# A fixed order for the first two SSD chunks, and other staging buffers for late weights, in a hybrid SSD and attention block

## The chip, the cores and the metric

The kernel runs on one NeuronCore of one Trainium2 chip. The metric is device time in microseconds of one launch, the median of several. The core has five instruction streams that run side by side: TensorE (PE in the profile, its weight loads PEld), VectorE (DVE), ScalarE (ACT), GpSimd (POOL) and SyncE (SP), which issues most DMAs. Each engine takes its instructions strictly in the order in which they stand in its queue, and waits on semaphores for the others.

## The reference

One encoder layer over a sequence of 1024 rows of width 1024, batch 1, all float32. The input is normalised and modulated (scale and shift from a conditioning vector), then one projection feeds two mixers of width 512 each: a Mamba-2 SSD group and a chunked attention group. Their outputs are concatenated, go through W_out, are gated and added; a feed-forward block with a depthwise convolution follows, then a last norm. The change is in the SSD mixer and in what surrounds it:

```python
xbc = jax.nn.silu(causal_dwconv(xbc, conv_w) + conv_b)      # x (512), B (256), C (256)
dt = jax.nn.softplus(dt_raw + dt_bias);  A = -jnp.exp(a_log)
y = ssd_scan(xs * dt[..., None], dt * A, bm, cm)            # decay masks exp(segment sums), states
y = y + d_skip[:, None] * xs
y = y.reshape(b, s, SSD_WIDTH) * jax.nn.silu(z)
y_ssd = rmsnorm(y, norm_w)
x = x + g_m * (jnp.concatenate([y_ssd, y_att], axis=-1) @ w_out)
```

## The kernel before

Float32 products run as three fp32r matmuls of a high and a low part (mm3); the function split makes the two parts of a tile, the high one on ScalarE and the low one on VectorE. After attention come the convolutions of x, B and C (tiles xst, bt, ct), then z's projection in two passes of 260 columns (ch 1, then ch 0), eight row tiles of 128 each, then the SSD in eight chunks of 128 rows.

**z.** wz_weights(ch) loads a pass's weights in four pieces into the two halves of raws (raw_tile hands them out in turn) and splits each into wzh and wzl, of which there are four buffers, so a pass's pieces are replaced as the pass before ends. z_mm makes a row tile (24 matmuls), z_evac writes zs. Between the tiles of the second pass stand, in an order written by hand, the preparation of the decays (dt_prep: sm_p, sm_e, sm_t, dt, adh and adl; dt_sums: running sums on TensorE, tile tp), the masks of chunks 0 and 1, and the splits of W_out's eight slots (wout_split, tiles hH and hL), staged in wos and raws.

**SSD.** For a chunk, pre_x scales x (xdt, xdd), pre_rm makes the decay mask's operands (tile rm, two buffers, "mask buffers"), pre_sg sums them on TensorE (sg), pre_cb makes C times B and B's transpose (xps to cb), and pre_m takes the exponential of sg on ScalarE and multiplies by cb on VectorE (tile th). ssd_y then makes y: on TensorE ydp (from th and xdt), yop (from the state) and stp (the next state), on VectorE the sum of ydp and GpSimd's yy, the products with the decays and with zs; ScalarE squares it, GpSimd makes the root, ScalarE scales y, and ssd_turn transposes it back into xs, which is half of W_out's input. wout_half(n) multiplies one half of a row tile by W_out (tile wops; n even is attention's half, from ya, n odd the SSD's, from xs), after wout_rhs has split that half into yhl. In chunk c the half c fills TensorE's time while the masks of chunk c+1 are made.

**What sets the order.** TensorE's order from z's second pass to the last chunk is that of the code. On VectorE and ScalarE a scheduler in the compiler sets the order, by its own estimate of the times; only where V.on and A.on are set does every instruction come after the one before it in the code. Before the change that part ends inside chunk 0: the two engines' instructions after ssd_y(0) are the scheduler's. GpSimd and SP are always the scheduler's.

```python
y = ssd_y(c, *pre)
V.on = A.on = False
if turn:
    ssd_turn(*turn)
```

Of the kernel before, what the change touches and what calls it, by code (L numbers as in the profile page):

```python
# [10 lines left out]
F32 = mybir.dt.float32  # L11
F32R = mybir.dt.float32r
# [4 lines left out]
P = 128  # L17
# [47 lines left out]
def tile_block(ctx: ExitStack, tc: tile.TileContext, x, crep, pk, w_ada, w_first, w_ft, w_z,  # L65
# [14 lines left out]
    def split(hi, lo, src, ehi, elo, scale=None):  # L80
        if scale is not None:
            A.activation(hi, src, AF.Copy, scale=scale)
            V.scalar_tensor_tensor(lo, src, scale, f32(hi), op0=ALU.mult, op1=ALU.subtract)
            return
        i = A.activation(hi, src, AF.Copy) if ehi is A else ehi.tensor_copy(hi, src)  # L85
        return i, elo.tensor_tensor(lo, src, f32(hi), ALU.subtract)  # L86
# [19 lines left out]
    def stat(n=1):  # L106
        if stc[0] + n > 64:
            stc[0] = 0
        a = st1[:, stc[0]:stc[0] + n]
        stc[0] += n  # L110
        return a

    def rstd(ms, eps=EPS):
        n = ms.shape[-1]
        r = stat(n)
        G.tensor_scalar(ms, ms, eps, None, op0=ALU.add)
        G.tensor_tensor(r, ms, mhalf[:, 0:n], ALU.pow)
        return r
# [8 lines left out]
    def raw_tile(n=1024):  # L127
        rawc[0] += 1
        return raws[:, rawc[0] % 2, 0:n]
# [499 lines left out]
    def wz_weights(ch):  # L629
        ws = []  # L630
        for a in range(4):
            th_ = wzp.tile([P, 2, 288], F32R, tag="wzh", bufs=WZB, name="wzh")[:, :, 0:260]
            tl_ = wzp.tile([P, 2, 288], F32R, tag="wzl", bufs=WZB, name="wzl")[:, :, 0:260]
            t = raw_tile(520)
            nc.sync.dma_start(t, w_z[ch, :, a * 520:(a + 1) * 520])
            split(th_, tl_, t.rearrange("p (a b) -> p a b", a=2), A, V, scale=0.5)
            ws.append((th_, tl_))
        return ws

    def z_mm(ch, st, wz):  # L640
        if st % 4 > 1:
            ps = psv.tile([P, 512], F32, tag=("acc", "pv")[st % 4 - 2], bufs=1, name="zps")[:, 0:260]
        else:
            ps = s_tile()[:, 0:260]
        for kt in range(KT):
            mm3(ps, hth[st // 4][:, st % 4, kt, :], htl[st // 4][:, st % 4, kt, :],
                wz[kt // 2][0][:, kt % 2, :],
                wz[kt // 2][1][:, kt % 2, :], kt == 0, kt == KT - 1)
        return ps
# [121 lines left out]
    def wout_get(*slots):  # L771
        for j in slots:
            wt[j] = wout_load(*WORDER[j])
# [11 lines left out]
            wout_fold(wt[j])  # L785
    wz = wz_weights(0)
    wout_get(5, 2)
    V.on = A.on = T.on = True
    V.last = A.last = T.last = None
    zp = z_mm(0, 0, wz)  # L790
# [56 lines left out]
    def sg_tile():  # L847
        return ps2a.tile([P, 512], F32, tag="seg", bufs=PB[2], name="sg")
# [4 lines left out]
    def ssd_y(c, xdt, xdd, cb, ms_):  # L853
        cs = slice(c * P, (c + 1) * P)
        prev, cur = state[c % 2], state[(c + 1) % 2]
        ydp = ssd_tile("ydp")
        for h in range(8):
            pe(T.matmul, ydp[:, h * 64:h * 64 + 64], ms_[h // 4][:, h % 4, :],
               xdt[:, h * 64:h * 64 + 64], start=True, stop=True)
        y = sp.tile([P, 512], F32, tag="yy", bufs=2, name="yy")  # L860
        G.tensor_tensor(h8(y), h8(xs[:, c, :]),
                        pkt[:, DSK:DSK + 8].unsqueeze(2).to_broadcast([P, 8, 64]), ALU.mult)
        t = sp.tile([P, 512], F32, tag="yt", bufs=2, name="yt")
        if c > 0:
            yop = ssd_tile("yop")
            for g in range(2):
                pe(T.matmul, yop[:, g * 256:g * 256 + 256], ct_[g][:, cs], prev[:, g * 256:g * 256 + 256],
                   start=True, stop=True)
        if c < NT - 1:
            stp = ssd_tile("stp")  # L870
            for g in range(2):
                pe(T.matmul, stp[:, g * 256:g * 256 + 256], cb[:, 2 + g, :],
                   xdd[:, g * 256:g * 256 + 256], start=True, stop=True)
            if c > 0:
                G.tensor_tensor(h8(cur), h8(prev), hb("cd", c), ALU.mult)
                V.tensor_tensor(cur, stp, cur, ALU.add)
            else:
                A.activation(cur, stp, AF.Copy)
        V.tensor_tensor(y, ydp, y, ALU.add)
        if c > 0:  # L880
            V.tensor_tensor(h8(t), h8(yop), hb("ea", c), ALU.mult)
            V.tensor_tensor(y, y, t, ALU.add)
        V.tensor_tensor(y, y, zs[:, c, 0:512], ALU.mult)
        ms = stat()
        A.activation(t, y, AF.Square, accum_out=ms)
        r = rstd(ms, 512.0 * EPS)
        A.activation(y, y, AF.Copy, scale=r)
        return y

    def ssd_turn(c, y):  # L890
        tps = x_tile()
# [17 lines left out]
            for j, g in enumerate(names):  # L909
                gd[g, m] = t[:, :, j, :]  # L910

    mod_scale(affn, SC_F, NFFN, 0, KT)
    mod_shift(bffn, SH_F, 0, KT)
    xr_, yq, wps, xrs = {}, {}, {}, []

    def wout_rhs(st, part):
        if st < NT:
            y = yq[st, part] = wu.tile([P, 2, 4, P], F32R, tag="wh", name="yhl")
            split(y[:, 0], y[:, 1], x1[part][:, st, :].rearrange("p (a b) -> p a b", a=4), A, V)

    def wout_half(n, ks=slice(0, 8), fill=()):
        st, part = n // 2, n % 2
# [58 lines left out]
    pre, turn = pre0, None  # L981
    T.on = False
    chain[:] = [T.last]
    for c in range(NT):
        y = ssd_y(c, *pre)
        V.on = A.on = False
        if turn:
            ssd_turn(*turn)
        turn = (c, y)
        if c < NT - 1:  # L990
            pre = ssd_pre(c + 1, x_tile, sg_tile, lambda: wout_half(c, slice(0, 3)),
                          pre1 if c == 0 else None)
            row_scale(pin[0])
            wout_half(c, slice(3, 8))
        else:
            wout_half(c)
# [565 lines left out]
```

## Time and profile before

| | us |
|---|---|
| median of three runs (1216.84 to 1219.11) | 1217.25 |
| profiled execution, its own time | 1217.67 |
| its span, first to last instruction | 1215.9 |
| z's first pass ends, second begins | 394.6 |
| z's second pass ends, chunk 0 begins | 423.7 |
| chunk 2 begins | 451.0 |

The times in the profile count from the span's start. In a timeline row stand the start, the duration, the engine, the line, the operation and its tiles, and in brackets how long the engine had been idle and what released it; L58 is the helper that holds the order written by hand, so there the tile tells the place. A row of waits reads: engine and tile, the engine and tile waited for, total time, times, longest. In a table of stretches the clock is TensorE's granted clock, 1.00 being full speed.

### The profile page before, as it was taken

The numbers are of one execution on the slowest core, as the hardware profiler recorded it, in microseconds if no ns is written. First come the engines' busy times: TensorE is split into PE (matmuls) and PEld (weight loads), VectorE is DVE, ScalarE is ACT, GpSimd is POOL, SyncE is SP. The second block draws the span as 40 slices with busy tenths as digits, with TensorE's granted clock in tenths as the row PEclk, the third lists the DMA queues.
The fourth block names the chain that finished last, engine by engine and source line by source line (L and its number), as shares of the span: only waits on it lengthen the run. The fifth ranks groups of instructions, "written<-read, shape, count | busy, mean of one in ns | idle before, by whom it ended". The sixth has DMA issues, their size and how long they took to land.

```text
span 1215.9 us, 15656 instructions
## 1 busy us (share of the span) xinstructions
PE 1162.3 (96%) x5802; PEld 976.8 (80%) x5802; DVE 942.3 (77%) x1413; ACT 594.9 (49%) x1001; POOL 195.2 (16%) x174
## 2 busy tenths in 40 slices
PE   5999999999999989999899999999999999999995
PEld 4887888778889978888688888888888888888884
DVE  7756455598697788747899988988889779766976
ACT  4637465663333657676454543444434445433443
POOL 1109373782210134200000000000000000000002
PEclk9999999999999999999999999999999999999998
DMA  9632121323554301141223223322333278733533
GB/s 355 237 94 83 36 74 39 129 81 127 174 174 157 104 18 36 61 147 53 70 80 129 96 104 130 118 81 87 105 130 112 91 265 293 261 118 125 169 117 138
DMA packets 56683, 151.91 MB, mean 125 GB/s; under 512 B 5664, under 2 KB 5792, under 8 KB 55200
## 3 DMA queue, kind: packets, MB, share of 16 engines
q1 hardware_dynamic: 49552, 126.54, 31.3%
q10 hardware_dynamic: 7056, 24.38, 5.0%
q8 instruction: 45, 0.74, 0.3%
q14 instruction: 30, 0.25, 0.1%
HBM read 117.61 MB, written 29.10 MB: 121 GB/s over the span
## 4 chain that ended last, share of the span: by engine, by line
PE 67%; DVE 7%; ACT 2%; DMA 1%; issue 1%; POOL 0%; DVEq 0%; POOLq 0%; SPq 0%; ACTq 0%
PE dn L76 6%; PE dn L77 6%; PE dn L78 6%; PE wops L702 6%; PE uY L76 5%; PE uY L78 5%; PE uY L77 5%; PE uZ L78 3%; PE uZ L77 3%; PE uZ L76 3%; PE uX L78 3%; PE uX L77 3%; PE uX L76 3%; PE s L76 2%; PE s L77 2%; PE s L78 2%
## 5 line engine op out<-in xcount | busy, mean ns | idle before, releaser
L978 POOL TENSOR_TENSOR st<-st,mhalf 128x1 f32<-128x1 f32 x16 | 12.7, 799 | 691.7 <-DVE st L977 680.3
L76 PE MATMUL dn<-w 128*128 128x512 f32 x308 | 111.9, 389 | 0.0
L77 PE MATMUL dn<-w 128*128 128x512 f32 x308 | 111.9, 389 | 0.0
L78 PE MATMUL dn<-w 128*128 128x512 f32 x308 | 103.3, 389 | 0.0
L76 PE MATMUL uY<-tH,w 128*128 128x512 f32 x256 | 99.7, 390 | 1.8 <-ACT w L58 1.8
L410 POOL TENSOR_SCALAR p<-p,st 128x640 f32<-128x640 f32 (+4 forms) x64 | 98.5, 1554 | 13.6 <-DVE st L409 10.4
L78 PE MATMUL uY<-tH,w 128*128 128x512 f32 x256 | 99.6, 389 | 0.0
L77 PE MATMUL uY<-tL,w 128*128 128x512 f32 x256 | 99.6, 389 | 0.0
L85 ACT ACTIVATE w<-ya 128x1024 fp32r<-128x1024 f32 (+1 forms) x41 | 39.1, 955 | 86.1 <-PE uY L78 80.8
L702 PE MATMUL wops<-hH,yhl 128*128 128x512 f32 x224 | 74.9, 403 | 2.6 <-ACT yhl L85 1.4
L78 PEld LDWEIGHTS dn<-w 128*128 128x128 f32 x308 | 57.8, 188 | 12.1
L76 PEld LDWEIGHTS dn<-w 128*128 128x128 f32 x308 | 57.8, 188 | 12.0
L77 PEld LDWEIGHTS dn<-w 128*128 128x128 f32 x308 | 57.8, 188 | 11.9
L85 ACT ACTIVATE pt<-tp 128x512 fp32r<-128x512 f32 (+2 forms) x72 | 36.6, 523 | 48.6 <-PE tp L436 19.7
L404 DVE CUSTOM_DVE_ANT_0 p<-s,bias 128x640 f32<-128x640 f32 (+4 forms) x64 | 40.6, 650 | 25.4 <-PE tp L439 8.5
L86 DVE TENSOR_TENSOR pt<-tp,pt 128x512 fp32r<-128x512 f32 (+2 forms) x72 | 41.9, 595 | 22.3 <-ACT pt L85 13.4
L76 PEld LDWEIGHTS uY<-tH,w 128*128 128x128 f32 x256 | 48.0, 188 | 12.1 <-ACT w L58 2.2
L77 PEld LDWEIGHTS uY<-tL,w 128*128 128x128 f32 x256 | 48.1, 188 | 10.0
L78 PEld LDWEIGHTS uY<-tH,w 128*128 128x128 f32 x256 | 48.1, 188 | 9.9
L85 ACT ACTIVATE w<-xs 128x1024 fp32r<-128x1024 f32 (+1 forms) x41 | 38.9, 952 | 32.4 <-PE uY L78 32.4
L702 PEld LDWEIGHTS wops<-hH,yhl 128*128 128x128 f32 x224 | 42.4, 191 | 11.9 <-ACT yhl L85 1.7
L76 PE MATMUL s<-hH,wh 128*128 128x512 f32 x128 | 50.6, 395 | 0.9 <-DVE ct L515 0.9
(472 smaller groups left out, 3426.8 us busy)
## 6 DMA issues: line engine op xcount, KB each, us to landing
gz<-a ACTq DMA_DIRECT2D x10, 1024.0 KB, 5.3
wos<-in_w_ada_dram SPq DMA_DIRECT2D x18, 512.0 KB, 4.1
ya<-in_w_up_dram SPq DMA_DIRECT2D x11, 768.0 KB, 4.2
xs<-in_w_up_dram SPq DMA_DIRECT2D x11, 768.0 KB, 4.4
adat<-in_w_ada_dram SPq DMA_DIRECT2D x16, 512.0 KB, 6.4
raws<-in_w_ft_dram SPq DMA_DIRECT2D x16, 512.0 KB, 3.6
qk<-in_w_ada_dram SPq DMA_DIRECT2D x14, 512.0 KB, 4.4
gy<-a ACTq DMA_DIRECT2D x10, 512.0 KB, 2.6
```

Of the source, the lines that this page charges most:

```text
L76: T.matmul(ps, lh, rh, start=start, stop=False, skip_group_check=more)
L77: T.matmul(ps, lh, rl, start=False, stop=False, skip_group_check=more)
L78: T.matmul(ps, ll, rh, start=False, stop=stop, skip_group_check=more)
L85: i = A.activation(hi, src, AF.Copy) if ehi is A else ehi.tensor_copy(hi, src)
L86: return i, elo.tensor_tensor(lo, src, f32(hi), ALU.subtract)
L404: V.tensor_tensor_reduce(out=dst, in0=src, in1=bsl, scale=-1.0, scalar=3e38, op0=ALU.add, op1=ALU.min, accum_out=nm)
L410: G.tensor_scalar(pv_, pv_, rr, None, op0=ALU.mult)
L702: i = op(*a, **k)
L978: G.tensor_tensor(r, ms, mhalf[:, 0:1], ALU.pow)
```

## The change

Four edits, all between the convolutions and chunk 2.

1. z's second pass stages its pieces 2 and 3 in the mask buffers (tag rm, name wzt) instead of the raws halves that pieces 0 and 1 use.
2. The three small operations that make affn and bffn stand earlier in the code, where the scheduler still sets the order.
3. The split of attention's first half (wout_rhs(0, 0)) joins the order written by hand, before slot 5's; slots 6 and 7 of W_out leave it there and come in chunk 0, behind parts of y.
4. Chunks 0 and 1 are written out in a fixed order for VectorE and ScalarE too. y's square and scale are separate functions, so that the exponential of the next chunk's first mask can stand ahead of the square; chunk 0 is turned inside its own chunk, its W_out half is cut at 3 and 6; in the fixed part the state's sum comes after y's.

```diff
+            if ch == 0 and a > 1:
+                t = bcp.tile([P, S], F32, tag="rm", bufs=2, name="wzt")[:, 0:520]
+            else:
+                t = raw_tile(520)
...
+    mod_scale(affn, SC_F, NFFN, 0, KT)
+    mod_shift(bffn, SH_F, 0, KT)
...
     zp = z_mm(0, 7, wz)
+    wout_rhs(0, 0)
     wout_split(5, wt[5])
     z_evac(0, 7, zp)
-    for j in (6, 7):
-        wout_split(j, wt[j])
...
+    def ssd_sq(y, t):
         ms = stat()
         A.activation(t, y, AF.Square, accum_out=ms)
-        r = rstd(ms, 512.0 * EPS)
+        return rstd(ms, 512.0 * EPS)
+
+    def ssd_scale(y, r):
         A.activation(y, y, AF.Copy, scale=r)
         return y
...
-    for c in range(NT):
-        y = ssd_y(c, *pre)
-        V.on = A.on = False
+    y, t = ssd_y(0, *pre)
+    wout_split(6, wt[6])
+    sg = pre_sg(pre1[0], sg_tile())
+    cb = pre_cb(1, x_tile())
+    wout_half(0, slice(0, 3))
+    m0 = pre_m(0, sg, cb)
+    r = ssd_sq(y, t)
+    wout_split(7, wt[7])
+    sg = pre_sg(pre1[1], sg_tile())
+    y = ssd_scale(y, r)
+    m1 = pre_m(1, sg, cb)
+    pre = *pre1["x"], cb, [m0, m1]
+    pre2 = {"x": pre_x(2), 0: pre_rm(2, 0)}
+    wout_half(0, slice(3, 6))
+    ssd_turn(0, y)
+    wout_rhs(0, 1)
+    pre2[1] = pre_rm(2, 1)
+    wout_half(0, slice(6, 8))
+    y, t = ssd_y(1, *pre)
+    sg = pre_sg(pre2[0], sg_tile())
+    cb = pre_cb(2, x_tile())
+    wout_half(1, slice(0, 3))
+    m0 = pre_m(0, sg, cb)
+    r = ssd_sq(y, t)
+    sg = pre_sg(pre2[1], sg_tile())
+    m1 = pre_m(1, sg, cb)
+    turn = 1, ssd_scale(y, r)
+    V.on = A.on = False
+    pre = *pre2["x"], cb, [m0, m1]
+    wout_half(1, slice(3, 8))
+    for c in range(2, NT):
+        y = ssd_norm(*ssd_y(c, *pre))
         if turn:
             ssd_turn(*turn)
```

ScalarE where z's first pass ends and the second begins, before (zt is z_evac's, wzh the weights, sm_e and na dt_prep's):

```order
L654 ACTIVATE zt<-zps 128x260
L82 ACTIVATE wzh<-raws 128x2x260 x2
L654 ACTIVATE zt<-zps 128x260
L82 ACTIVATE wzh<-raws 128x2x260
L58 ACTIVATE sm_e<-sm_p 128x64
L58 ACTIVATE na<-pkt 128x8
L82 ACTIVATE wzh<-raws 128x2x260
L58 ACTIVATE adh<-sm_e 128x64
```

and with the change:

```order
L657 ACTIVATE zt<-zps 128x260
L82 ACTIVATE wzh<-raws 128x2x260 x2
L82 ACTIVATE wzh<-wzt 128x2x260
L657 ACTIVATE zt<-zps 128x260
L82 ACTIVATE wzh<-wzt 128x2x260
L58 ACTIVATE sm_e<-sm_p 128x64
L58 ACTIVATE na<-pkt 128x8
L58 ACTIVATE adh<-sm_e 128x64
```

The two late pieces stand ahead of dt_prep's first exponential, and no longer on both sides of it.

VectorE from the last z tile on, before (hL slots 6 and 7 of W_out, cb and th the masks of chunk 1, yy the y of chunk 0):

```order
L58 SCALAR_TENSOR_TENSOR zs<-zt,zps 128x260
L709 TENSOR_TENSOR xdt<-xs,sm_dt 128x512
L58 SCALAR_TENSOR_TENSOR hL_86<-wos,pkt,hH_84 128x512 x2
L719 TENSOR_TENSOR rm<-tle_2879,adl 128x512
L58 SCALAR_TENSOR_TENSOR hL_86<-raws,pkt,hH_84 128x512
L740 TENSOR_TENSOR cb<-xps,tle_2879 128x512
L58 SCALAR_TENSOR_TENSOR hL_86<-raws,pkt,hH_84 128x512
L58 TENSOR_TENSOR st_72<-modc,pkt 128x8
L748 TENSOR_TENSOR th<-th,cb 128x512 x2
L58 SCALAR_TENSOR_TENSOR affn<-st_72,pkt 128x8
L58 TENSOR_TENSOR bffn<-modc,pkt 128x8
L58 TENSOR_TENSOR yy<-ydp,yy 128x512
```

and with the change:

```order
L58 SCALAR_TENSOR_TENSOR zs<-zt,zps 128x260
L58 TENSOR_TENSOR yy<-ydp,yy 128x512
L58 TENSOR_TENSOR yy<-yy,zs 128x512
L58 SCALAR_TENSOR_TENSOR hL_86<-wos,pkt,hH_84 128x512 x2
L58 TENSOR_TENSOR cb<-xps,tle_2879 128x512
L58 TENSOR_TENSOR th<-th,cb 128x512
L58 SCALAR_TENSOR_TENSOR hL_86<-raws,pkt,hH_84 128x512 x2
L58 TENSOR_TENSOR th<-th,cb 128x512
L58 TENSOR_TENSOR xdt<-xs,sm_dt 128x512
L58 TENSOR_TENSOR rm<-tle_2879,adl 128x512
L58 TENSOR_TENSOR yhl<-xs,yhl 128x512
```

y of chunk 0 comes first and slots 6 and 7 after it, between the masks; xdt and rm of chunk 2 come after the masks of chunk 1.

ScalarE in chunk 0, before (state the chunk's state, th<-sg the exponentials, yt the square and the second yy the scale of y):

```order
L58 ACTIVATE hH_84<-wos,pkt 128x512 x2
L58 ACTIVATE hH_84<-raws,pkt 128x512 x2
L58 ACTIVATE state_4137<-stp 128x512
L747 ACTIVATE th<-sg 128x512
L717 ACTIVATE rm<-tle_2879,adh 128x128 x4
L747 ACTIVATE th<-sg 128x512
L717 ACTIVATE rm<-tle_2879,adh 128x128 x4
L723 ACTIVATE rm<-tle_2879,adl 128x128 x4
L58 ACTIVATE yt,st_72<-yy 128x512
L58 ACTIVATE yy<-yy,st_72 128x512
```

and with the change:

```order
L58 ACTIVATE state_4137<-stp 128x512
L58 ACTIVATE hH_84<-wos,pkt 128x512 x2
L58 ACTIVATE th<-sg 128x512
L58 ACTIVATE yt,st_72<-yy 128x512
L58 ACTIVATE hH_84<-raws,pkt 128x512 x2
L58 ACTIVATE yy<-yy,st_72 128x512
L58 ACTIVATE th<-sg 128x512
L58 ACTIVATE rm<-tle_2879,adh 128x128 x4
L58 ACTIVATE xs<-xps 128x512
L58 ACTIVATE yhl<-xs 128x512
```

The square and the scale of y stand among the splits and exponentials of chunk 0 instead of behind all of chunk 2's rm. On GpSimd the third yy (chunk 2's) now stands ahead of chunk 2's xdd. From chunk 2's ydp on every engine has the same order as before.

More of the change, by code (lines that the diff above doesn't have):

```diff
@@ L633, in wz_weights @@
             tl_ = wzp.tile([P, 2, 288], F32R, tag="wzl", bufs=WZB, name="wzl")[:, :, 0:260]
-            t = raw_tile(520)
+            if ch == 0 and a > 1:
+                t = bcp.tile([P, S], F32, tag="rm", bufs=2, name="wzt")[:, 0:520]
+            else:
+                t = raw_tile(520)
             nc.sync.dma_start(t, w_z[ch, :, a * 520:(a + 1) * 520])
@@ L787, in tile_block, with wout_rhs @@
     wout_get(5, 2)
+    mod_scale(affn, SC_F, NFFN, 0, KT)
+    mod_shift(bffn, SH_F, 0, KT)
+    yq = {}
+    def wout_rhs(st, part):
+        if st < NT and (st, part) not in yq:
+            y = yq[st, part] = wu.tile([P, 2, 4, P], F32R, tag="wh", name="yhl")
+            split(y[:, 0], y[:, 1], x1[part][:, st, :].rearrange("p (a b) -> p a b", a=4), A, V)
     V.on = A.on = T.on = True
@@ L875, in ssd_y @@
                 G.tensor_tensor(h8(cur), h8(prev), hb("cd", c), ALU.mult)
-                V.tensor_tensor(cur, stp, cur, ALU.add)
+                if not V.on:
+                    V.tensor_tensor(cur, stp, cur, ALU.add)
             else:
@@ L882, in ssd_y, with ssd_norm @@
             V.tensor_tensor(y, y, t, ALU.add)
+            if V.on:
+                V.tensor_tensor(cur, stp, cur, ALU.add)
         V.tensor_tensor(y, y, zs[:, c, 0:512], ALU.mult)
+        return y, t
+    def ssd_sq(y, t):
         ms = stat()
         A.activation(t, y, AF.Square, accum_out=ms)
-        r = rstd(ms, 512.0 * EPS)
+        return rstd(ms, 512.0 * EPS)
+    def ssd_scale(y, r):
         A.activation(y, y, AF.Copy, scale=r)
         return y
+    def ssd_norm(y, t):
+        return ssd_scale(y, ssd_sq(y, t))
     def ssd_turn(c, y):
@@ L910, in tile_block @@
                 gd[g, m] = t[:, :, j, :]
[L912 to L919, printed above, removed]
+    xr_, wps, xrs = {}, {}, []
     def wout_half(n, ks=slice(0, 8), fill=()):
@@ L990, in tile_block @@
         if c < NT - 1:
-            pre = ssd_pre(c + 1, x_tile, sg_tile, lambda: wout_half(c, slice(0, 3)),
-                          pre1 if c == 0 else None)
+            pre = ssd_pre(c + 1, x_tile, sg_tile, lambda: wout_half(c, slice(0, 3)))
             row_scale(pin[0])
```

## The prediction

> **What bounds the kernel now.** I read the page's head first, then TensorE's waits around the edit (340 to 470 us), then the busy time by stretch, and last the timelines of the engines, from which rows are picked out below.
>
> ```profile
> span 1215.9 us, 15656 instructions
> PE 1162.3 (96%) x5802; PEld 976.8 (80%) x5802; DVE 942.3 (77%) x1413; ACT 594.9 (49%) x1001; POOL 195.2 (16%) x174
> PE wops L702 <- ACT yhl L85: 1.4, 1, 1.4
> PE xps L702 <- ACT yy L58: 1.2, 1, 1.2
> PE wops L702 <- DVE yhl L86: 1.1, 1, 1.1
> PE s L58 <- ACT wzh L82: 1.1, 1, 1.1
> PE ydp L702 <- DVE th L748: 0.4, 1, 0.4
> PE s L58 <- DVE wzl L83: 0.3, 1, 0.3
> ```
>
> TensorE is busy 96% of the span, so an edit pays only where TensorE waits or is clocked down. These six waits lie at two places: z's second pass (tile s) and the SSD's second chunk (ydp, xps, wops).
>
> ```profile
> 394.58:404.16 9.58, 8.10 (x51) 7.48 (x49) 6.75 (x24) 3.21 (x10) 0.00 (x0) 0.82 0.51 167
> 398.75:402.50 3.75, 3.73 (x19) 3.52 (x18) 3.34 (x14) 0.00 (x0) 0.00 (x0) 0.55 0.82 271
> 404.16:423.69 19.53, 19.53 (x162) 19.36 (x161) 13.16 (x20) 15.56 (x39) 2.09 (x2) 1.00 0.25 82
> 423.69:433.58 9.89, 9.89 (x56) 8.29 (x54) 9.89 (x14) 8.10 (x21) 5.08 (x4) 1.00 0.00 1
> 433.58:451.00 17.42, 13.26 (x64) 10.60 (x64) 12.38 (x19) 9.32 (x24) 5.93 (x7) 0.90 0.04 16
> 444.06:447.09 3.03, 3.03 (x8) 2.41 (x9) 1.15 (x2) 0.72 (x1) 0.90 (x2) 0.53 0.00 0
> 451.00:462.00 11.00, 11.00 (x63) 9.62 (x62) 10.39 (x14) 5.84 (x16) 5.68 (x6) 1.00 0.06 24
> 462.00:473.01 11.01, 11.01 (x64) 9.62 (x63) 8.72 (x12) 7.28 (x21) 4.34 (x6) 1.00 0.16 49
> ```
>
> Columns: stretch, length, busy time of PE, PEld, DVE, ACT, POOL, granted clock, DMA. A chunk without waits lasts 11.0 us; the second lasts 17.42, with TensorE idle for 4.2 and its clock at 0.53 for 3 us after the waits. VectorE is busy through all of chunk 0 (9.89 of 9.89): it does the last W_out splits ahead of y, and chunk 1 pays. In z the first two tiles of the second pass are 48 matmuls; at the 0.12 us between the z matmuls after them (24 to a tile, six tiles with their small insertions in 19.53) they need 5.76 and take 9.58.
>
> **z's late weights.** What sets them now:
>
> ```profile
> 389.87 0.60 ACT L146 ACTIVATE rows<-rowps 128x512 f32<-128x512 f32 x1 [1.31 <-PE rowps L145]
> 394.02 1.05 SPq L635 DMA_DIRECT2D raws<-in_w_z_dram  x2
> 394.79 0.39 ACT L654 ACTIVATE zt<-zps 128x260 f32<-128x260 f32 x1 [0.80 <-PE zps L78]
> 396.62 0.64 ACT L82 ACTIVATE wzh<-raws 128x520 fp32r<-128x520 f32 x1 [1.44 <-DMA raws<-in_w_z_dram]
> 397.16 0.24 ACT L58 ACTIVATE sm_e<-sm_p 128x64 f32<-128x64 f32 x1
> 397.90 0.19 DVE L58 TENSOR_SCALAR sm_t<-sm_e 128x64 f32<-128x64 f32 x1
> 398.91 0.55 DVE L58 RECIPROCAL sm_t<-sm_t 128x64 f32<-128x64 f32 x1
> 402.54 0.22 DVE L58 SCALAR_TENSOR_TENSOR sm_e<-sm_dt,na 128x64 f32<-128x64 f32 x1
> 404.16 0.33 PE L58 MATMUL tp<-sm_e,tle 128*128 128x64 f32 x2
> ```
>
> The late loads are issued at 394.02, when a raws half is free, and land 2.6 us later; TensorE waits for them. The mask buffers are free when the last row product has been read by TensorE (before 389.87), so the second load can land near 392.6, ahead of its use at 394.8. On SP the two loads pass only the issue of gfd; the W_out loads behind them come earlier, not later. Their wzh buffers come free as the last tile of the first pass ends at 394.7. So ScalarE makes the fourth wzh right after zt, 395.1 to 395.7, VectorE its wzl by 396.5 (0.70), and matmul 19 of the new tile, at 394.58 + 18 x 0.12 = 396.74, finds it. Both tiles then end at 394.58 + 5.76 = 400.34.
>
> What is late next is the decay chain (dt_prep), which stood behind the weights on both engines. sm_e moves from 397.16 to 396.85, since VectorE's sm_p now follows wzl; no wzl cuts into the chain, so from sm_e's end it takes 0.04 + 0.22 + (402.76 - 398.91 = 3.85) = 4.1: ready at 401.2. TensorE wants it at 400.34 and waits 0.9. The running sums therefore start at 401.25 and not 404.16: **-2.9**. Bounds: -3.8 if the chain is not waited for, -1.4 if the clock falls again (16 matmuls at twice 0.12 cost 1.5 before, 398.75 to 402.50). After that TensorE was not held between 404.16 and 423.69, and VectorE and ScalarE, 1.5 ahead instead of 2.9, catch up by their own idle time there (13.16 and 15.56 busy of 19.53).
>
> **The two SSD chunks.** If nothing waited, chunks 0 and 1 would take 9.89 + 11.0 = 20.9 from 423.69 on instead of 27.31: at most -6.4. Against that stands VectorE's queue, with GpSimd's in its way:
>
> ```profile
> 422.33 1.41 DVE L58 SCALAR_TENSOR_TENSOR hL<-wos,pkt,hH 128x512 fp32r<-128x512 f32 x2
> 424.82 1.49 POOL L861 TENSOR_TENSOR yy<-xs,pkt 128x512 f32<-128x512 f32 x1
> 425.33 1.52 DVE L58 SCALAR_TENSOR_TENSOR hL<-raws,pkt,hH 128x512 fp32r<-128x512 f32 x1
> 434.64 0.68 DVE L58 TENSOR_TENSOR yy<-ydp,yy 128x512 f32<-128x512 f32 x1
> 436.14 0.63 ACT L58 ACTIVATE yt<-yy 128x512 f32<-128x512 f32 x1 [3.00 <-DVE yy L58]
> 438.12 1.04 POOL L710 TENSOR_TENSOR xdd<-xdt,ex 128x512 f32<-128x512 f32 x1
> 438.19 0.72 ACT L58 ACTIVATE yy<-yy,st 128x512 f32<-128x512 f32 x1 [1.32 <-POOL st L117]
> 438.53 1.18 DVE L882 TENSOR_TENSOR yy<-yy,yt 128x512 f32<-128x512 f32 x1
> ```
>
> A split of half a W_out tile is 0.70 alone and 1.52 beside GpSimd's yy; the sum yy<-yy,yt, 0.68 else, is 1.18 and ends 0.55 after GpSimd's xdd. One waits for the other's end. So I walk the new order with 0.6 to 0.7 per 512-wide VectorE operation, 1.04 per GpSimd operation, in turns where both want to run; times on the old clock, with z's end at 423.69.
>
> VectorE, from zs of z tile 6 (ends 424.1): yhl and slot 5's halves behind GpSimd's first two yy, to 427.8; zs; y's sum and product, 429.5; slot 6, 430.7; cb 431.3; first mask product 432.3, behind GpSimd's power; slot 7, 433.6; second mask product 435.2, behind GpSimd's third yy, which the turn has released; xdt, rm, 436.4; yhl 438.0, behind xdd; y of chunk 1 with xdt and the state, 441.5 (0.5 blocked); rm 442.1; y's product 443.75, behind the state's decay; cb, yhl 444.95; first mask product 446.0 (0.4 blocked); xr; second 447.2. ScalarE: y's square from 429.5, GpSimd's two operations (1.32 from square to scale before, a little more behind VectorE's slot 6), scale at 432.45, the exponential behind it 433.0.
>
> ```profile
> 423.69 1.89 PE L702 MATMUL ydp<-xdt,th 128*128 128x64 f32 x16
> 430.00 0.40 PE L702 MATMUL wops<-hH,yhl 128*128 128x512 f32 x1
> ```
>
> TensorE needs the scaled y at 432.07 (in chunk 0 the second sg is past at 430.0, then nine wops of 0.23): waits 0.4. The second mask product of chunk 1 is needed by ydp's second half only (eight of its 16 passes, 0.87), at 423.69 + 9.89 + 0.36 (the moved turn) + 0.4 + 0.87 = 435.2: none. Chunk 2's first is needed at 423.69 + 20.9 + 0.4 = 445.0 and comes at 446.0: waits 1.0; its second, needed at 446.9, waits 0.3. The splits of yhl are ready a microsecond before their wops. Sum of new waits 1.7, so -6.4 + 1.7 = **-4.7**. Bounds: -6.4, if GpSimd's turns fall between VectorE's operations (the blocked turns add to some 6 us by then), and -3.2, if the clock falls once as at 444.06, where 3.03 us at 0.53 cost 1.4 to 1.5. I take the walk, since the blocked turns are in the rows. Every instruction that moved is in it; none was added or removed.
>
> **The three affine operations** go from chunk 0 into the convolution.
>
> ```profile
> 330.82 0.47 PE L76 MATMUL s<-hH,wh 128*128 128x512 f32 x1 [0.87 <-DVE ct L515]
> 433.21 0.15 DVE L58 TENSOR_TENSOR st<-modc,pkt 128x8 f32<-128x8 f32 x1
> 433.28 1.28 DVE L748 TENSOR_TENSOR th<-th,cb 128x512 f32<-128x512 f32 x2
> 331.00:335.00 4.00, 4.00 (x19) 3.29 (x19) 3.56 (x5) 2.97 (x4) 2.72 (x2) 1.00 0.60 230
> ```
>
> Two of them now stand ahead of the ct that TensorE waits for at 330.82. Each takes 0.07 of VectorE's time (433.21 to 433.28): **+0.15**, bounds 0 and +0.3 (their full 0.15). The third takes the place of yhl's split, 0.6 longer, so the later xst comes no later.
>
> Sum: +0.15 - 2.9 - 4.7 = -7.45. The profiled execution took 1217.67 us (span 1215.9): 1210.2. The median of the runs, 1217.25, is 0.4 lower: **1209.8 us**. Later stages keep their order on every engine and only start earlier.
>
> A rule that bears on this: the clock fell after waits of 1.1 and 0.3, with some dispatch time around them, and stayed at 1.00 after the single 0.87 at 330.82. [...]
>
> **Rivals.**
> (a) Both chains keep ahead of TensorE: -3.8 - 6.4 + 0.15 = -10.05, 1207.2. For it: VectorE's idle time after 404; against it: 9.89 of 9.89 and 10.39 of 11.00 busy in chunks 0 and 2. 13%.
> (b) The clock falls after a new wait at one place: 1.5 back, 1211.3; at both, 1212.8. For it: the waits at ydp of chunk 2 come as two, 1.0 and 0.3, like those in z. Against: 0.87 alone did nothing. 17%.
> (c) The edit in z doesn't do what it says: the mask buffers' loads, held for the last row product, come no earlier than 396.6. Then -4.7 + 0.15, 1212.7. For it: SP takes loads in order, so one held load holds the next; against: 389.87 is four microseconds before 394.02. 7%.
> (d) Slower: from chunk 2 on VectorE's loop, mask product to mask product, sets the chunk. Before, VectorE entered chunk 2 rested by chunk 1's waits; now it enters late. The row of 451.00 has 0.61 spare, and TensorE waited 0.56 for y at 488.62 already. If a chunk grows from 11.0 to more than 12.5, the six chunks 2 to 7 (five full intervals) give back 7.5; at 13.0 they cost 10, 1219.8. Against: the row of 462.00 has 2.3 spare, so lateness drains within a chunk or two. 4%.
>
> ```profile
> 488.62 0.55 PE L702 MATMUL xps<-ident,yy 128*128 128x128 f32 x3 [0.56 <-ACT yy L887]
> ```
>
> (e) New waits eat more than half of the gain in some other way, 1214 to 1216: 4%. The forecast itself, 1208.5 to 1211, has 55%.
>
> The bounds add to -10.2 and -4.3, 1207.0 to 1213.0; runs of before lie between 1216.84 and 1219.11, so the upper end gets one more: **1207.0 to 1214.0**, which leaves out (d), (e) and the edges of (a), below 2 in 10. With 0.2% (2.4 us, about what a measurement of this kernel tells from no change) as the bound: faster 0.91 (forecast, a, b and most of c), same 0.05, slower 0.04.
>
> **What would show it.** z: no wait of s on wzh or wzl, one of the running sums' matmul (tp<-sm_e) on sm_e near 0.9, granted clock 1.00. SSD: from the first ydp to chunk 2's ydp about 22.6 us instead of 27.31, no wait on yhl, waits on yy (0.4) and th (1.3). Convolution: the wait at 330.82 near 1.0. Wrong would be: a clock under 0.9 in either stretch, a wait that recurs in chunks 3 to 6, or loads of wzt that land after 394.8.

## The result, and the profile after

The changed kernel takes 1210.27 us (median of six runs, 1209.32 to 1211.91) against 1217.45 (six runs, 1216.84 to 1221.3): ratio 0.9937, 95% interval 0.9923 to 0.995. The profiled execution took 1210.66, its span is 1208.9; 1209.8 was forecast.

TensorE's waits of the changed kernel, those of the convolution first, then those from z to chunk 5:

```profile
PE s L76 <- DVE ct L515: 1.1, 1, 1.1
PE tp L594 <- DVE xst L521: 0.7, 1, 0.7
PE tp L58 <- DVE sm_e L58: 0.8, 1, 0.8
PE xps L705 <- ACT yy L906: 0.6, 1, 0.6
```

The six waits of before are gone. One on the decay chain (sm_e) has come, as foretold. The waits foretold on yy at chunk 0's turn and on th before chunk 2 aren't listed. The last one belongs to chunk 5 and was there before. The stretches of the changed kernel (columns as before: length; busy PE, PEld, DVE, ACT, POOL; clock):

```profile
395.66:402.39 6.73, 5.93 (x51) 5.72 (x49) 5.75 (x21) 1.41 (x6) 0.00 (x0) 1.00 0.50 159
422.03:443.12 21.09, 21.01 (x119) 17.84 (x117) 20.92 (x29) 15.18 (x39) 10.87 (x11) 1.00 0.00 1
443.12:454.54 11.42, 11.33 (x63) 9.80 (x64) 11.39 (x16) 8.41 (x23) 6.06 (x7) 1.00 0.12 46
```

z's second pass needs 6.73 us to the running sums where it needed 9.58, the two chunks 21.09 where they needed 27.31, chunk 2 takes 11.42 where it took 11.00. These three give -2.85 - 6.22 + 0.42 = -8.65; the spans differ by 7.0. The rest went the other way. TensorE reaches z's second pass 1.08 later (395.66 against 394.58): 0.7 of it is there already at 239 us, where both kernels run the same instructions, and 0.27 comes from the convolution's wait on ct, ahead of which two of the moved operations now stand. From the running sums to the first ydp it takes 0.1 longer, from chunk 3 to the end 0.5. What the 0.7 is, the runs below showed.

z's late weights on SyncE's queue and ScalarE, and the matmul that now waits:

```profile
387.80 4.30 SPq L638 DMA_DIRECT2D wzt<-in_w_z_dram  x2
395.14 0.64 ACT L82 ACTIVATE wzh<-wzt 128x520 fp32r<-128x520 f32 x1
396.14 0.63 ACT L82 ACTIVATE wzh<-wzt 128x520 fp32r<-128x520 f32 x1
402.39 0.43 PE L58 MATMUL tp<-sm_e,tle 128*128 128x64 f32 x2 [0.80 <-DVE sm_e L58]
```

The loads are issued from 387.8 on instead of at 394.02, and the fourth split ends at 396.77, while the second pass began at 395.66.

GpSimd and VectorE from chunk 0 to the start of chunk 2 of the changed kernel, from the two timelines:

```profile
425.55 1.21 POOL L886 TENSOR_TENSOR state<-state,ex 128x512 f32<-128x512 f32 x1 [0.91 <-ACT state L58]
431.20 1.27 POOL L872 TENSOR_TENSOR yy<-xs,pkt 128x512 f32<-128x512 f32 x1 [1.61 <-PE xps L705]
433.70 1.42 POOL L713 TENSOR_TENSOR xdd<-xdt,ex 128x512 f32<-128x512 f32 x1 [1.23 <-DVE xdt L58]
439.29 1.42 POOL L886 TENSOR_TENSOR state<-state,ex 128x512 f32<-128x512 f32 x1 [1.23 <-DVE state L58]
...
426.12 0.68 DVE L58 TENSOR_TENSOR yy<-ydp,yy 128x512 f32<-128x512 f32 x1
431.48 1.53 DVE L58 TENSOR_TENSOR th<-th,cb 128x512 f32<-128x512 f32 x1
434.14 1.52 DVE L58 TENSOR_TENSOR yhl<-xs,yhl 128x512 fp32r<-128x512 f32 x1
439.73 1.53 DVE L58 TENSOR_TENSOR yy<-yy,zs 128x512 f32<-128x512 f32 x1
442.38 0.68 DVE L58 TENSOR_TENSOR th<-th,cb 128x512 f32<-128x512 f32 x1
443.59 0.68 DVE L58 TENSOR_TENSOR th<-th,cb 128x512 f32<-128x512 f32 x1
```

Each long row of VectorE ends 0.54 to 0.55 us behind the end of the GpSimd row that began ahead of it (433.01 after 432.47, 435.66 after 435.12, 441.26 after 440.71). The row at 426.12 began under a GpSimd row too and is not long; its first input, ydp, lies in PSUM, while the long ones read two tiles in SBUF. The last two rows are chunk 2's mask products. The walk had them end at 446.0 and 447.2 on the old clock, which is 444.3 and 445.5 on this one; they end at 443.06 and 444.27. TensorE starts ydp at 443.12, with 0.08 us idle in all of the two chunks ahead of it. Inside ydp it loses 0.4 more, for the second product: its 16 passes take 2.30 there and 1.89 in chunk 3.

The scaled y at chunk 0's turn, on ScalarE and then on TensorE:

```profile
429.62 0.72 ACT L58 ACTIVATE yy<-yy,st 128x512 f32<-128x512 f32 x1
430.40 0.66 PE L705 MATMUL xps<-ident,yy 128*128 128x128 f32 x4
```

It is ready at 430.34, and TensorE, which takes it at 430.40, does not wait.

### The profile page after: what moved, and what is told of

It reads as the page before. It is cut to its first block, busy times and chain, and to the rows that moved or that the text cites. A ratio compares the mean times of both kernels' runs of the same rounds, so it can differ in the third digit from the quotient of the medians.

```text
span 1208.9 us, 15656 instructions
## 1 busy us (share of the span) xinstructions
PE 1159.7 (96%) x5802; PEld 974.6 (81%) x5802; DVE 941.8 (78%) x1413; ACT 594.7 (49%) x1001; POOL 195.3 (16%) x174
## 4 chain that ended last, share of the span: by engine, by line
PE 67%; DVE 7%; ACT 2%; issue 1%; DMA 1%; POOL 0%; SPq 0%; DVEq 0%; POOLq 0%; ACTq 0%
PE dn L76 6%; PE dn L77 6%; PE dn L78 6%; PE wops L705 5%; PE uY L76 5%; PE uY L78 5%; PE uY L77 5%; PE uZ L78 3%; PE uZ L77 3%; PE uZ L76 3%; PE uX L78 3%; PE uX L77 3%; PE uX L76 3%; PE s L76 2%; PE s L77 2%; PE s L78 2%
## 5 line engine op out<-in xcount | busy, mean ns | idle before, releaser
L78 PEld LDWEIGHTS dn<-w 128*128 128x128 f32 x308 | 57.8, 188 | 12.1
L76 PEld LDWEIGHTS uY<-tH,w 128*128 128x128 f32 x256 | 48.0, 188 | 12.1 <-ACT w L58 2.2
L86 POOL TENSOR_TENSOR wl<-raws,wh 128x1024 fp32r<-128x1024 f32 x14 | 36.2, 2589 | 93.5 <-ACT wh L85 93.3
```

The costliest lines, as they stand in the source:

```text
L76: T.matmul(ps, lh, rh, start=start, stop=False, skip_group_check=more)
L78: T.matmul(ps, ll, rh, start=False, stop=stop, skip_group_check=more)
```

## The experiments

All kernels were timed beside the kernel before on the same chip; its medians there were 1217.67, 1218.78 and 1218.7 in the three groups of runs. Times across groups are compared by their ratios to it.

### The change in z alone

```diff
 before.py, wz_weights:
-            t = raw_tile(520)
+            if ch == 0 and a > 1:
+                t = bcp.tile([P, S], F32, tag="rm", bufs=2, name="wzt")[:, 0:520]
+            else:
+                t = raw_tile(520)
```

> The kernel before with the staging of z's last two weights in the mask buffers alone; the SSD's order is the old one. Theory 1 (the z term stands by itself): from the start of the second pass's first new tile to the running sums' matmul 6.7 us as in the changed kernel instead of 9.58, so 1217.45 - 2.85 = 1214.6; one wait of that matmul on sm_e of 0.8, clock 1.00 there; chunk 1's waits stay as they were (17.4 us from its first ydp to the next). Theory 2 (z's gain is eaten by the SSD, since VectorE enters chunk 0 less rested): the stretch is 6.7 as well, but chunks 0 and 1 together take more than 28.5 instead of 27.31, and the time is 1216 or more. Theory 3 (a wait of 0.8 can close the gate): clock below 0.9 in the stretch, 1216.1.

Measured: 1216.4 (1213.56 to 1217.65, eleven runs), ratio 0.9984 (0.9973 to 0.9995), so 1.95 us gained, 0.6 to 3.3 by the interval. In the profile the stretch in z is 6.73, with the 0.8 wait at clock 1.00, as theory 1 had it. But the two chunks:

```profile
422.02:447.99 25.97, 21.79 (x118) 17.89 (x117) 22.29 (x32) 17.38 (x45) 11.01 (x11) 1.00 0.03 11
```

25.97 instead of 27.31, at a clock of 1.00, though the SSD's order is the old one and the same four waits stand in it (0.43, 1.17, 1.43, 1.15). No theory had that. The time is one that theories 2 and 3 had as well (1216 or more, 1216.1), but neither of their signs is there: the chunks are shorter and not longer, and the clock is 1.00. Why the time gained less than 2.85 stayed open here; the repeated executions below answer it.

### The SSD's order alone

```diff
 after.py, wz_weights:
-            if ch == 0 and a > 1:
-                t = bcp.tile([P, S], F32, tag="rm", bufs=2, name="wzt")[:, 0:520]
-            else:
-                t = raw_tile(520)
+            t = raw_tile(520)
```

> The changed kernel with z's last two weights staged as before; the SSD's order is the new one. Theory 1 (the SSD term is 5.8 and does not need z's): from the first ydp to chunk 2's ydp 21.1 us, chunk 2 11.4, the convolution 0.35 longer, so 1217.45 - 6.2 + 0.4 + 0.35 = 1212.0; z's stretch 9.6 at a clock near 0.82. Theory 2 (the rest that VectorE has from z's waits is what lets the new order run without waits, or its lack costs): the two chunks differ from 21.1 by more than 0.5. Theory 3 (my walk of the queues was right and the changed kernel's run a lucky one): 22.6 for the two chunks, 1213.1.

Measured: 1212.37 (1209.83 to 1213.3), ratio 0.9954 (0.9937 to 0.9971), 5.6 gained. The stretches:

```profile
396.89:405.28 8.39, 6.72 (x50) 5.89 (x48) 5.78 (x21) 1.90 (x5) 0.00 (x0) 1.00 0.59 189
424.93:446.00 21.07, 20.98 (x118) 17.82 (x116) 20.90 (x29) 15.15 (x39) 10.85 (x11) 1.00 0.00 1
```

Theory 1 holds for the SSD: 21.07, chunk 2 11.45. The new order needs nothing from z, and 5.6 + 1.95 = 7.55 is what both together gave (ratio 0.9937, 7.7). Theory 3, the walk as it stood, falls. And z's stretch is 8.39, not 9.6: the old weights' waits are there (1.13, 0.35 and one of 0.17), the clock stays at 1.00.

### The kernel before, twice more

Nothing edited. By then the low clock was the open question: with the same waits it fell in one execution and not in another. Profiles cut into stretches of 0.1 us show where each low stretch starts; the unit of the distances, 3.4133 us, is a 54th of the 184.32 us between the first and the last start in the profile of before:

| profile | starts of the low stretches, us | distances / 3.4133 |
|---|---|---|
| before | 399.14, 443.51, 583.46 | 13.0, 41.0 |
| after | 236.42, 577.76 | 100.0 |
| z alone | 95.81, 580.50 | 142.0 |
| splits first (below) | 236.34, 434.31, 581.09 | 58.0, 43.0 |
| sums early (below) | 236.69, 403.94, 581.44 | 49.0, 52.0 |

> The kernel before, unchanged, in another execution. Each low stretch of the clock so far lasted 3.3 to 3.5 us, and where an execution has several their starts lie a whole multiple of 3.413 us apart (44.37 is 13 of them, 139.95 is 41 in the first profile of before). Theory 1 (the clock is set for whole windows on a free-running grid, so whether a wait of 1 to 2 us costs it depends on how the wait lies to the grid): in this execution the same waits stand in z and in chunk 1, but the clock may stay at 1.00 in one or both; where it does, z's stretch is 8.4 instead of 9.58 (as in the run with z's old weights) and the two chunks 26.0 instead of 27.31 (as in the run with z's change alone). Theory 2 (the clock follows from the waits themselves): 9.58 and 27.31 again, with 0.5 at the same two places.

> The kernel before, unchanged, in a third execution, with the same expectations as the second: theory 1 (free-running grid) allows the low stretch at z and at chunk 1 to be there or not, 3.4 us long where it is there, starts a whole multiple of 3.413 us apart; theory 2 (the waits alone decide) has 9.58 and 27.31 as in the first.

Measured: 1217.59 and 1216.33. Theory 1, in both. The waits of the third execution, from TensorE's timeline:

```profile
398.71 0.39 PE L58 MATMUL s<-wzh,hH 128*128 128x260 f32 x1 [1.13 <-ACT wzh L82]
438.93 0.66 PE L702 MATMUL xps<-ident,yy 128*128 128x128 f32 x4 [1.17 <-ACT yy L58]
442.14 0.50 PE L702 MATMUL wops<-hH,yhl 128*128 128x512 f32 x1 [1.44 <-ACT yhl L85]
444.02 0.73 PE L702 MATMUL wops<-hH,yhl 128*128 128x512 f32 x2 [1.15 <-DVE yhl L86]
```

Its stretches around z's second pass (which runs from 395.98) and over the two chunks:

```profile
394.00:404.00 10.00, 8.47 (x66) 7.86 (x66) 7.33 (x24) 3.08 (x7) 0.00 (x0) 1.00 0.50 157
423.64:449.63 25.99, 21.80 (x119) 17.89 (x118) 22.30 (x32) 17.44 (x45) 10.98 (x11) 1.00 0.03 11
```

The waits are those of the first profile to 0.03 us (1.11, 1.16, 1.42 and 1.15 there), the clock is 1.00 at both places; z takes 8.02 (8.44 in the second execution, with 1.26 for the first wait), the two chunks 25.99 in both. The first profile of before, cut at the low stretches' own starts, with the 3.41 us ahead of each:

```profile
395.73:399.14 3.41, 1.93 (x12) 1.31 (x11) 1.98 (x6) 1.52 (x4) 0.00 (x0) 1.00 0.28 95
399.14:402.55 3.41, 3.41 (x16) 3.41 (x17) 2.96 (x14) 0.00 (x0) 0.00 (x0) 0.50 0.91 301
440.10:443.51 3.41, 1.39 (x8) 0.72 (x7) 3.38 (x4) 3.41 (x10) 2.16 (x2) 1.00 0.00 0
443.51:446.92 3.41, 2.86 (x7) 2.28 (x8) 1.70 (x3) 0.77 (x2) 1.31 (x2) 0.50 0.00 0
```

The same for the run with the splits first, below:

```profile
430.90:434.31 3.41, 0.46 (x5) 0.46 (x5) 1.30 (x3) 1.95 (x5) 1.15 (x2) 1.00 0.00 0
434.31:437.72 3.41, 3.41 (x13) 2.84 (x11) 3.40 (x4) 3.38 (x11) 2.38 (x2) 0.50 0.00 0
```

The clock is 0.50 for one whole window and back at 1.00 behind it (in before from 402.55 and from 446.92 on). Ahead of these three stands a window in which TensorE was busy for 1.93, 1.39 or 0.46 us of 3.41. Half of 3.41 makes 1.7 us the most that a low window can cost, by estimate, and with the same waits it comes in one execution and not in another. The 0.7 at 239 us in the first profile of the changed kernel is such a window too (236.42 to 239.83, clock 0.50), in code that is the same in both kernels. A low window near there is in eleven of the fourteen profiles; the first profile of before, from which the prediction was worked, is one of the three without it.

What brings a low window the runs don't settle. In the changed kernel the window ahead of the low one at 236.42 had only 1.13 us of idle time. A window with 1.85 us, in the run of the next section, was followed by one at full clock:

```profile
233.01:236.42 3.41, 2.28 (x16) 1.59 (x14) 3.02 (x11) 3.36 (x10) 3.08 (x3) 1.00 0.88 308
439.20:442.61 3.41, 1.56 (x7) 0.94 (x6) 3.41 (x6) 0.83 (x4) 1.42 (x1) 1.00 0.00 0
442.61:446.02 3.41, 2.81 (x12) 2.33 (x13) 2.48 (x4) 2.58 (x8) 1.47 (x2) 1.00 0.00 0
```

So neither the length of a wait nor the idle share of one window decides alone. The idle share counts for something: in all fourteen profiles, without their first and last 20 us, six windows held less than 1.5 us of TensorE's work (1.39 and 0.46 above and 1.35 in the run with the sums early are three of them), and each was followed by a low one.

### Square ahead of the exponential

```diff
 after.py, chunks 0 and 1:
-    m0 = pre_m(0, sg, cb)
     r = ssd_sq(y, t)
+    m0 = pre_m(0, sg, cb)
```

> The changed kernel with y's square (and the root behind it) put ahead of the first exponential in chunks 0 and 1 on ScalarE; no other engine's order changes. Theory 1 (ScalarE has slack at both places, the late splits are what mattered): in chunk 0 the square waits for y at 427.6 as before, the exponential (0.58) and the split behind it come after it, the scaled y is up to 0.5 later than TensorE's turn; in chunk 1 the first exponential falls behind the square that VectorE's y holds until 441.3, and the first mask product is 0.2 later. Together 0.5 to 0.8: 1210.8 to 1211.1. Theory 2 (the exponentials ahead of the square carry the SSD's gain): TensorE waits again on th for over a microsecond, the clock falls, 1213 or more.

Measured: 1213.82 (1212.68 to 1215.09), ratio 0.9958 (0.9944 to 0.9971), 2.5 above the changed kernel's 0.9937. Theory 2, but not by the wait on th that either theory had looked at:

```profile
429.44 0.73 PE L705 MATMUL sg<-rm,sgtr 128*128 128x512 f32 x2 [0.83 <-ACT th L58]
443.21 0.74 PE L705 MATMUL sg<-rm,sgtr 128*128 128x512 f32 x2 [2.44 <-ACT th L58]
...
441.95 0.63 ACT L58 ACTIVATE yt<-yy 128x512 f32<-128x512 f32 x1 [2.58 <-DVE yy L58]
442.58 0.58 ACT L58 ACTIVATE th<-sg 128x512 f32<-128x512 f32 x1
```

sg has a single buffer in PSUM. The chunk's second mask sum can only be written when the first exponential has read the first one, and that exponential now stands behind a square that waits for VectorE's y until 441.95. TensorE stands still for 2.44 us, and the two chunks take 24.63 instead of 21.09 (chunk 2 is back at 11.00), 3.1 more in all. The clock didn't fall here: it is 1.00 over the 24.63 us.

### The late splits ahead of y

```diff
 after.py, chunk 0:
+    for j in (6, 7):
+        wout_split(j, wt[j])
     y, t = ssd_y(0, *pre)
-    wout_split(6, wt[6])
...
-    wout_split(7, wt[7])
```

> The changed kernel with the last two W_out splits ahead of the first y on ScalarE and VectorE, as they were before; the rest of the new order stays. Theory 1 (the late splits ahead of y are what makes the first y late): VectorE does 2.8 us of splits before y's sum, the scaled y is some 2.8 late at TensorE's turn, of which about 2.5 is waited for; with a wait that long the clock may fall for another 1.5: 1212.8, or 1214.3 with the clock. VectorE's total work up to chunk 2's mask product is the same, so part of this can come back there (VectorE is busy throughout, and chunk 2's start hangs on it): not less than 1211.5. Theory 2 (the splits' place does not matter, since the queue's total sets chunk 2's start): 1210.3, with the waits only moved.

Measured: 1214.08 (1212.67 to 1215.56), ratio 0.996 (0.9946 to 0.9973), 2.8 above the changed kernel. Theory 1, with its clock window, in the profiled execution (1215.0):

```profile
433.85 0.72 PE L705 MATMUL xps<-ident,yy 128*128 128x128 f32 x4 [3.31 <-ACT yy L58]
```

One wait of 3.31, then the low window shown above; the chunks take 14.91 and 10.99. Chunk 2 takes 11.00 again, so 0.42 comes back there and no more. Both parts of the new order carry weight: undone singly, each costs 2.5 to 2.8 us by the ratios. The other parts (attention's first split ahead of slot 5, the state's sum behind y's, chunk 0 turned inside its own chunk) were not undone singly.

### GpSimd's products on VectorE

```diff
 after.py:
-        G.tensor_tensor(h8(y), h8(xs[:, c, :]), ...          # D times x
+        (V if c < 2 else G).tensor_tensor(h8(y), h8(xs[:, c, :]), ...
-        G.tensor_tensor(h8(xdd), h8(xdt), hb("de", c), ALU.mult)
+        (V if c == 2 else G).tensor_tensor(h8(xdd), h8(xdt), hb("de", c), ALU.mult)
-                G.tensor_tensor(h8(cur), h8(prev), hb("cd", c), ALU.mult)
+                (V if c == 1 else G).tensor_tensor(h8(cur), h8(prev), hb("cd", c), ALU.mult)
```

> The changed kernel with four of GpSimd's 512-wide products of chunks 0 to 2 (D times x of chunks 0 and 1, the decay of the state in chunk 1, xdd of chunk 2) done by VectorE itself. Theory 1 (an operation of GpSimd holds VectorE up: the VectorE operations of 1.4 to 1.5 us beside them are 0.68 of work and 0.75 to 0.85 of waiting): VectorE gets four more operations of 0.60, and loses three such holds of 0.74 to 0.84: 2.4 against 2.36, so the two chunks stay at 21.1 within 0.4, time 1210 to 1210.7, and the VectorE operations beside the removed ones take 0.68. Theory 2 (GpSimd runs beside VectorE at no cost to it, the long rows have another cause): the mask products of chunk 2 come 2.4 later, the two chunks take 23.3, time 1212.5.

Measured: 1208.75 (1207.96 to 1210.93), ratio 0.9915 (0.9901 to 0.9929). The two chunks, chunk 2, chunk 5:

```profile
423.38:444.16 20.78, 20.78 (x119) 17.91 (x117) 20.45 (x33) 16.29 (x44) 4.86 (x6) 1.00 0.00 1
444.16:455.94 11.78, 11.35 (x63) 9.80 (x63) 10.75 (x15) 7.69 (x19) 6.58 (x8) 1.00 0.12 45
477.95:488.96 11.01, 11.01 (x63) 9.62 (x62) 8.93 (x12) 7.43 (x22) 4.58 (x5) 1.00 0.16 49
```

Theory 1: with four more operations VectorE has as much time left as before (20.78 + 11.78 = 32.56 against 32.51), and yhl, 1.52 above, takes 0.68 at 435.37. So GpSimd's products weren't free: on average each cost VectorE about what VectorE itself needs for it. Chunk 5, which takes 12.08 in the changed kernel, takes 11.01: its wait of 0.55 on yy is gone. Neither theory had that, and its cause was not isolated. By the ratios this run is 2.7 us below the changed kernel, more than the stages show. At one granted clock, 0.994, five runs of it average 1208.6 and seven of the changed kernel 1209.9; these 1.3 are near chunk 5's 1.07.

### The running sums one tile earlier

```diff
 after.py, z's second pass:
+    dt_sums()
     zp = z_mm(0, 1, wz)
     r0 = pre_rm(0, 0)
-    dt_sums()
```

> The changed kernel with the running sums' matmuls issued one z tile earlier, behind the first tile of the second pass: TensorE then stands still in one piece for about 0.8 + 2.9 = 3.7 us. A look at the clock alone; the order of later stages shifts as well, so only z's stretch is read. Theory 1 (as the kernel before showed, waits of about 1 us following each other already close the gate, so a long one does): after the wait the clock is near half for some 3 us, and the tile behind the wait takes 1.5 more: from the tile's first matmul to the third tile's first 11.2 us. Theory 2 (a single wait does not close the gate, whatever its length up to 3.7): 9.6 us at 1.00.

One execution, 1215.04. TensorE stands still for 3.68 us in one piece and then:

```profile
400.53:403.94 3.41, 1.35 (x11) 1.35 (x12) 2.73 (x11) 0.96 (x4) 0.00 (x0) 1.00 0.02 5
403.94:407.35 3.41, 3.41 (x18) 3.41 (x17) 0.82 (x2) 1.06 (x4) 1.04 (x1) 0.50 0.01 2
```

Theory 1: a low window, though it starts 1.35 us after TensorE has gone on, at the window's end and not at the wait's. From the sums to the first ydp it takes 24.04 instead of 19.64 + 2.88 (the tile that comes later) = 22.52, so 1.5 for the clock. The window ahead of the low one began while TensorE still stood still.

### The running sums one tile later, and the small operations out of the convolution

```diff
 after.py, z's second pass (first kernel):
     r0 = pre_rm(0, 0)
-    dt_sums()
-    x0 = pre_x(0)
...
     zp = z_mm(0, 2, wz)
+    dt_sums()
+    x0 = pre_x(0)
 after.py (second kernel), from ahead of the second pass to its fifth tile:
-    mod_scale(affn, SC_F, NFFN, 0, KT)
-    mod_shift(bffn, SH_F, 0, KT)
...
     z_evac(0, 4, zp)
+    mod_scale(affn, SC_F, NFFN, 0, KT)
+    mod_shift(bffn, SH_F, 0, KT)
```

> The changed kernel with the running sums' three matmuls (and what reads them) issued one z tile later, so that TensorE has 24 more matmuls (2.9 us) before it needs the decay chain. Theory 1 (the 0.8 wait is pure loss): the wait on sm_e is gone, z's second pass to the first ydp is 0.8 shorter (25.6 instead of 26.37), 1209.5. Theory 2 (the chain behind the sums is late next): the first masks' exponentials or xdt come late, a new wait of 0.3 to 0.8 of TensorE before the first ydp, 1210.3 or a little more.

> The changed kernel with the three small operations on the feed-forward block's scale and shift placed behind the fifth tile of z's second pass, where VectorE has idle time, instead of in the convolution. Theory 1: the waits on ct (1.1) and xst (0.7) in the convolution go back to 0.87 and 0.6, which is 0.35 less from the convolution's start to z: 1209.9, nothing else moves. Theory 2 (the 0.35 is scatter between two executions): waits stay at 1.1 and 0.7, 1210.3. Theory 3 (VectorE has no 0.45 to spare before chunk 0): the second mask product of chunk 2 comes later, its wait grows by up to 0.45: 1210.3 as well, but with the convolution shorter.

Sums later: 1207.79 (1207.4 to 1210.0), ratio 0.9924 (0.9905 to 0.9942). From the second pass to the first ydp:

```profile
396.27:421.56 25.29, 25.29 (x211) 25.12 (x210) 19.88 (x43) 18.05 (x49) 2.09 (x2) 1.00 0.34 106
```

25.29 against 26.37, TensorE busy throughout: a wait shown as 0.80 was worth 1.08. No new wait came before the first ydp. Theory 1, by the stage; the intervals of the ratios overlap.

Small operations in z: 1209.74 (1209.28 to 1210.38), ratio 0.9937 (0.9922 to 0.9952), which isn't told from the changed kernel. The wait on ct is 0.90; over all profiles it is 0.77 to 0.87 with the operations in their old place (four) and 1.04 to 1.19 with them in the convolution (eight). The wait on xst is 0.84 here and between 0.51 and 0.87 elsewhere, whatever the kernel. Theory 1 for ct, theory 2 for xst: 0.2, not 0.35.

### All three, beside the changed kernel

> The changed kernel, unchanged, beside the combined version on one chip. z's stretch 6.73, the two chunks 21.1, chunk 2 11.4 whatever the execution (no wait left there that is long enough for the clock): 1210.3, ratio 0.9937. A profile without the low stretch near 236 us is 0.7 shorter before the convolution.

> The changed kernel with three edits together: the three small operations in z instead of the convolution, the running sums one z tile later, and the four products of GpSimd done by VectorE. If the gains add, by the stages of the single runs: -0.24 at the wait on ct, -1.08 in z (25.29 against 26.37 from the second pass to the first ydp), 0 in chunks 0 to 2 (32.56 against 32.51), -1.07 in chunk 5 (11.01 against 12.08): 2.4 under the changed kernel, 1207.9. In the feed-forward block the order of some work shifts with it, as it did in the run with the early sums, where it cost nothing. Rival: the wait of chunk 5 comes back, since which of GpSimd's operations meets which of VectorE's depends on when z ends: 1209.

The changed kernel: 1210.12 (1209.73 to 1211.67), ratio 0.9933 (0.9921 to 0.9946); 6.73, 21.09 and 11.42 again. All three: 1208.56 (1206.57 to 1210.47), ratio 0.992 (0.9906 to 0.9933). Its stretches (z, the two chunks, chunk 5):

```profile
395.26:420.55 25.29, 25.29 (x211) 25.12 (x209) 20.20 (x46) 18.06 (x49) 2.09 (x2) 1.00 0.34 106
420.55:441.35 20.80, 20.80 (x119) 17.91 (x117) 20.47 (x33) 16.33 (x44) 4.91 (x6) 1.00 0.00 1
475.10:486.11 11.01, 11.01 (x64) 9.62 (x63) 8.94 (x12) 7.49 (x22) 4.58 (x5) 1.00 0.15 49
```

Stage by stage the gains add as expected, and chunk 5's wait did not come back. In time it is 1.6 us of the 2.4; the two intervals overlap, so by the times alone the combined version isn't proved faster than the changed kernel.

## Why the prediction came out right

1209.8 against 1210.27. What the change takes away and what it leaves was foretold in kind, but that the total came within 0.5 us is in part luck: two terms were mis-sized, and the base held something that isn't the kernel's.

**The base.** The working took 9.58 and 27.31 as what z and the two chunks cost before. In that execution they held two low windows: z takes 8.0 to 8.4 without one, the chunks 25.98. Two executions without a low window in either stretch (the third of before, span 1214.6, and the second of the changed kernel, span 1208.2) give the clean account:

| | forecast | first profiles | without low windows |
|---|---|---|---|
| the convolution's wait on ct | +0.15 | +0.27 | +0.28 |
| z's second pass to the first ydp | -2.9 | -2.74 | -1.29 |
| chunks 0, 1 and 2 | -4.7 | -5.80 | -4.48 |
| sum | -7.45 | -8.27 | -5.5 |

The spans of the clean pair differ by 6.40; the rest of that is a low window near 582 us that only the one has (-1.21 from chunk 3 to the end), and +0.3 elsewhere.

So the clean gain is 5.5, and the times gained 7.2 (medians) to 7.7 (ratio). The granted clock on record for every timed run shows where most of the rest comes from. One low window is 0.0014 of it (half of 3.41 in 1217 us). The kernel before averages 0.9910 over the 35 runs timed beside the experiments, the changed one 0.9934 over eleven: before, an execution holds between one and two low windows more, by that estimate. At one granted clock, 0.993, ten runs of before average 1217.2 and three of the changed kernel 1211.1, which is 6.1. The forecast booked both low windows of one profile in full. On average the old order does pay most of that, but the prediction had no reason to count on it.

**z, -2.9.** The step was right in every part that the rows show: the loads in time, no wait on wzh or wzl, the chain next, its wait 0.8 for 0.9, the stretch 2.85 shorter than in the profile used. Mis-sized was the -2.9 as a gain of the kernel: it is 1.3 to 1.7 where the clock holds. The bound's "16 matmuls at twice 0.12 cost 1.5" is a slip (that would be 1.9; the row's 3.75 less its 19 matmuls at 0.12 gives 1.5). Rival (c), that the edit does nothing, fell.

**The two chunks, -4.7.** The step that failed is "sum of new waits 1.7". By the profile used the term was -6.22, with 0.08 of waiting left, and 0.42 behind it in chunk 2: 0.5 and not 1.7. The walk gave VectorE 0.6 to 0.7 per operation and some 6 us of blocked turns. The rows show one operation each 0.60 us and six holds of 0.42 to 0.85, 4.5 in all. Chunk 2's mask products were 1.3 earlier than walked, the scaled y at chunk 0's turn in time. That a blocked turn is the cost of GpSimd's products stood up (with them on VectorE, yhl takes 0.68 and not 1.52). With GpSimd under way, yy<-ydp at 426.12, which reads a PSUM tile, was not held (0.68, against the 1.52 to 1.53 of the rows that read two tiles in SBUF); the walk had not told the two apart. Without the low window the term is -4.9, or -4.5 with chunk 2; there the forecast was near for the wrong reason, since its -6.4 held 1.3 of clock and its waits were 1.2 too many.

**The convolution, +0.15.** The wait on ct grew by 0.27, the upper bound: the operations cost their full 0.15 each on the way to ct, not 0.07.

**The rivals.** (a), (d) and (e) did not come. Against (d): chunks 3 to 6 take 11.0, 11.1, 12.1 and 11.0 in both kernels, so VectorE's late entry drains within chunk 2. (b), the clock after a new wait: no profile shows a fall at the 0.8 wait (clock 1.00 from 395.66 to 402.39). But the prediction's picture of the clock was wrong. It asked how long a wait is; in the profiles the clock is 0.50 for whole windows of 3.41 us, whose starts lie whole multiples of 3.4133 apart, to a hundredth of a window. The window ahead of a fall need not be one of waiting alone: TensorE was busy for 1.93 us of it ahead of one and for 2.28 ahead of another.

## What to carry to other kernels

A profile is one execution: before a stall is priced, look whether the clock was down behind it, and take the stretch from a second execution, or the price of a clock window that comes in one execution and not in another (1.3 us in the two chunks here) is booked as the edit's gain. In a stage where VectorE is full, count how long GpSimd's work holds it up (4.5 us in the two chunks here), and walk the queue with the spacing of rows, not with their lengths; where a PSUM tile has one buffer, its reader's place in its queue decides when TensorE may go on (2.44 us on sg here). An edit that takes a wait away can be worth more than the idle time shown (0.80 shown and 1.08 gained in z, 0.55 and 1.07 in chunk 5).

## What was not expected of the hardware

The clock was 0.50 for whole windows of 3.41 us on a grid that runs through an execution (starts 13.0, 41.0, 49.0, 52.0, 58.0, 100.0 and 142.0 windows apart); of two executions with the same waits, to 0.03 us, one lost 1.3 us to it in the SSD and the other nothing. And four operations of 0.60 us moved from GpSimd to a VectorE that was busy for 20.9 of 21.1 us left the three chunks as long as they were (32.56 against 32.51).
